# Seven-product SwiGLU pairs: silu and weight splits placed behind the PSUM copies in the queues of ScalarE and VectorE

## The chip, the cores and the metric

The kernel runs on one core of a Trainium2 chip. The metric is the device time of one execution in microseconds. A core has five engines with queues of their own, each working through its queue in order: TensorE (PE, with PEld for its weight loads), VectorE (DVE), ScalarE (ACT), GpSimd (POOL) and SyncE (SP), which issues the loads.

## What is computed

The program is two blocks of two layers each over 512 tokens of width 1024. The change concerns the four SwiGLU feed-forward networks of the second block (two per layer), with a hidden width of 22 chunks of 128:

```
def _swiglu(h, w_gu, w_down):
    gate, up = jnp.split(h @ w_gu, 2, axis=-1)
    return (jax.nn.silu(gate) * up) @ w_down

x = _layer_norm(alpha * x + 0.5 * _swiglu(x, ...), ...)
mix = _token_mixers(x, ...)
x = _layer_norm(alpha * x + mix, ...)
x = _layer_norm(alpha * x + 0.5 * _swiglu(x, ...), ...)
```

## The kernel before, in words

All matmuls run at three products per weight tile (`mm3`, L488 to L490): a float32 weight is split into a high part `wh`, cast by ScalarE, and a low part `wl`, the rest, subtracted by VectorE (`split`, L472 and L473). Tiles with an x, xs or p in their names are activations split in the same way.

`swiglu` goes over the 22 chunks in three parts of 8, 8 and 6. The first four chunks of a SwiGLU (five in the first one) are computed plainly. Each other chunk is a "pair" (`gated`): the gate and up products of one chunk for both halves of the tokens, taken together with seven products instead of eight. There are 71 pairs: parts of 3, 8 and 6 in the first SwiGLU and of 4, 8 and 6 in the three others. After a part, eight accumulations project its result down (L1141).

The weights of a pair come from `strassen_w`. SyncE loads two halves, ra (`raw`, tag wr, three buffers, shared with the loads of the projections) and rb (L991, tag wr2, two buffers). GpSimd makes four sums in order: L995 (p1 = a21 + a22), L996 (p2), L998 (p3), L999 (p4). The first two fill tile c1, the others c2 (both tag wc, two buffers in all). L995 needs rb and a free wc buffer. Four splits follow: 11/12 straight from ra, p2/p1 from c1 (`wh`, `wl`), p3/p4 from c2 (`wh2`, `wl2`) and 22 from rb (`wh3`, `wl3`, one buffer).

The products of a pair, twelve matmuls each, accumulate in three PSUM tiles R, Z and Q. Product 11 goes into R and ScalarE copies it to e1 (L1028). Product 12 goes into Z; VectorE adds e1 to it (add g1, L1032) and ScalarE takes silu (L1023). Product p2 goes on into R, copied to e2 (L1037). Product p1 goes into Q; p3 into R, copied to e3 (L1043); VectorE makes n2 of e3 and Q (L1045). Product 22 goes on into R (L1051), p4 into Q; then come add g2 (L1054), silu g2 (L1023), a multiplication (L1056) and the split of the result into ph and pl (L472, L473).

Two pairs are interleaved: the generator of a pair is stepped together with that of the one before, so that TensorE's order for a pair k with j before it is 11(k), 12(k), 22(j), p2(k), p1(k), p4(j), p3(k). A scheduler orders every queue by its own estimates and by edges that the code adds (`issue_after`: an instruction is queued behind another on the same engine). Before, such edges put the p2/p1 split behind add g1 and e2 of the pair before, and the p3/p4 split behind its e3 and n2.

Of the kernel before, what the change touches and what calls it, by code (L numbers as in the profile page):

```python
# [13 lines left out]
ALU = mybir.AluOpType  # L14
# [7 lines left out]
H = T // 2  # L22
# [332 lines left out]
class Prog:  # L355
# [156 lines left out]

    def mac(self, W, X, cols=slice(0, T), tag=None, off=None):

        ps = self.pt(tag=tag) if tag else self.acc()
        o = ps[:, : cols.stop - cols.start]
        if off is not None:
            self.nc.tensor.matmul(o, self.mean[:], off[:, cols], start=True, stop=False)
        for k, (wh, wl) in enumerate(W):
            self.mm3(o, wh, wl, X[k][0][:, cols], X[k][1][:, cols], k == 0 and off is None, k == len(W) - 1)  # L520
        return ps
# [445 lines left out]

        return X1, scale, X, finish

    def strassen_w(self, sa, sb, behind):  # L970


        nc = self.nc
        out = {}

        def put(names, src, tags, bufs=2, pool=None, behind=()):
            n = len(names) * 512
            hi, lo = ((pool or self.pool).tile([P, n], F32R, tag=t, name=self.nm(t), bufs=bufs) for t in tags)
            with ExitStack() as ctx:
                for ins in behind:  # L980
                    ctx.enter_context(self.tc.issue_after(ins))
                self.split(src, hi[:], lo[:])
            for i, name in enumerate(names):
                out[name] = [
                    (hi[:, c : c + P], lo[:, c : c + P]) for c in range(i * 512, i * 512 + 512, P)
                ]

        ra = self.raw(sa, 1024)
        put(("11", "12"), ra[:], ("wh", "wl"), pool=self.main)
        rb = self.pool.tile([P, 1024], F32, tag="wr2", name=self.nm("wr2"), bufs=2)  # L990
        nc.sync.dma_start(rb[:], sb)  # L991
        a11, a12, a21, a22 = ra[:, :512], ra[:, 512:], rb[:, :512], rb[:, 512:]
        c1, c2 = (self.pool.tile([P, 1024], F32, tag="wc", name=self.nm("wc"), bufs=2) for _ in range(2))
        p2, p1, p3, p4 = c1[:, :512], c1[:, 512:], c2[:, :512], c2[:, 512:]
        nc.gpsimd.tensor_tensor(p1, a21, a22, op=ALU.add)  # L995
        nc.gpsimd.tensor_tensor(p2, p1, a11, op=ALU.add)  # L996
        put(("p2", "p1"), c1[:], ("wh", "wl"), pool=self.main, behind=behind[0])
        nc.gpsimd.tensor_tensor(p3, a11, a21, op=ALU.add)  # L998
        nc.gpsimd.tensor_tensor(p4, p2, a12, op=ALU.add)  # L999
        put(("p3", "p4"), c2[:], ("wh2", "wl2"), behind=behind[1])  # L1000
        put(("22",), a22, ("wh3", "wl3"), 1)
        return out

    def prod(self, ps, W, X, start):

# [7 lines left out]
    def gated(self, X, srcs, mid, tags):  # L1013

        nc = self.nc
        tr, tq, tz = tags  # L1020
        gv, hv = self.scratch()
        g1, g2, e1, n2 = gv[:, :H], gv[:, H:], hv[:, :H], hv[:, H:]
        silu = lambda t: nc.scalar.activation(t, t, AF.Silu)  # L1023
        W = self.strassen_w(*srcs, self.behind)
        self.behind = behind = [[], []]
        R = self.pt(tag=next(tr))
        self.prod(R, W["11"], X["11"], True)
        nc.scalar.copy(e1, R[:, :H])  # L1028
        yield
        Z = self.pt(tag=next(tz))  # L1030
        self.prod(Z, W["12"], X["21"], True)
        behind[0].append(nc.vector.tensor_tensor(g1, e1, Z[:, :H], op=ALU.add).ins)  # L1032
        silu(g1)
        yield
        e2, e3 = (self.pool.tile([P, H], F32, tag="u", name=self.nm("u"), bufs=3)[:] for _ in range(2))
        self.prod(R, W["p2"], X["nf"], False)
        behind[0].append(nc.scalar.copy(e2, R[:, :H]).ins)  # L1037
        yield
        Q = self.pt(tag=next(tq))
        self.prod(Q, W["p1"], X["d"], True)  # L1040
        yield
        self.prod(R, W["p3"], X["t3"], False)
        behind[1].append(nc.scalar.copy(e3, R[:, :H]).ins)  # L1043
        behind[1].append(
            nc.vector.scalar_tensor_tensor(  # L1045
                out=n2, in0=e3, scalar=-1.0, in1=Q[:, :H], op0=ALU.mult, op1=ALU.subtract
            ).ins
        )
        yield
        self.prod(R, W["22"], X["t4"], False)  # L1050
        nc.vector.scalar_tensor_tensor(out=g1, in0=R[:, :H], scalar=-1.0, in1=g1, op0=ALU.mult, op1=ALU.mult)  # L1051
        yield
        self.prod(Q, W["p4"], X["22"], False)
        nc.vector.tensor_tensor(g2, e2, Q[:, :H], op=ALU.add)  # L1054
        silu(g2)
        nc.vector.tensor_tensor(g2, g2, n2, op=ALU.mult)  # L1056
        pair = self.xpair("m")
        self.split(gv[:], pair[0][:], pair[1][:])
        mid.append(pair)

    def plain(self, srcs, X, mid, normed):

        nc = self.nc
        sg, bc = {}, None

        def evac(i, ps, cols):
            j, n = i // 2, cols.stop - cols.start
            if bc is not None:
                t = self.t("up", tag="m")
                nc.vector.tensor_tensor(t[:, :n], ps[:, :n], bc[:, cols], op=ALU.mult)  # L1070
                ps = t
            if i % 2 == 0:
                if j not in sg:
                    sg[j] = self.t("sg", tag="m")
                nc.scalar.activation(sg[j][:, cols], ps[:, :n], AF.Silu)
            else:
                if j == len(mid):
                    mid.append(self.xpair("m"))
                g = sg[j][:, cols]
                nc.vector.tensor_tensor(g, ps[:, :n], g, op=ALU.mult)  # L1080
                self.split(g, mid[j][0][:, cols], mid[j][1][:, cols])

        if normed is not None:
            X1, scale, X, finish = normed
            for i, ps in self.lagged(srcs, X1, 2):
                if bc is None:
                    bc = scale()
                    self.tail = finish(bc)
                evac(i, ps, slice(0, T))
                next(self.tail, None)  # L1090
        else:
            W = [self.weights(srcs[i], KC, None if i < 2 else ("wh2", "wl2")) for i in range(4)]

            def product(W, ps, t):
                for k in range(KC):
                    self.mm3(ps, *W[k], *X.block(k, t), k == 0, k == KC - 1)

            for t, cols in enumerate(HALVES):
                for i in range(4):
                    ps = self.acc()  # L1100
                    product(W[i], ps[:, :H], t)
                    evac(i, ps, cols)
                    if t == 0:
                        next(self.tail, None)
            for i in range(4, len(srcs)):
                W = self.weights(srcs[i], KC)
                ps = self.acc()
                for t, cols in enumerate(HALVES):
                    product(W, ps[:, cols], t)
                evac(i, ps, slice(0, T))  # L1110
                next(self.tail, None)
        for _ in self.tail:
            pass
        self.behind = [self.last] * 2
        return X

    def swiglu(self, x, X, l, s, out=None, form=None, normed=None):


        nc, I = self.nc, self.I  # L1120
        wg = I[f"wg{l}{s}"]
        tags = cycle(("acc", "acc")), cycle(("s", "s")), cycle(("t", "t"))
        for a, b in PARTS:
            mid, j0 = [], a
            if a == 0:
                j0 = NPLAIN + (normed is not None)
                X = self.plain([wg[i * FC + j] for j in range(j0) for i in range(2)], X, mid, normed)
            before = iter(())
            for j in range(j0, b):
                g = self.gated(X, (wg[j], wg[FC + j]), mid, tags)  # L1130


                for one in (g, g, before, g, g, before, g):
                    next(one, None)
                before = g
            for _ in before:
                pass
            if b < FC:
                for nb in range(KC):
                    ps = self.proj(I[f"we{l}{s}"][nb][:, a * P : b * P], mid, b - a)  # L1140
                    nc.vector.scalar_tensor_tensor(  # L1141
                        out=x[nb][:], in0=ps[:], scalar=0.5 / ALPHA, in1=x[nb][:], op0=ALU.mult, op1=ALU.add
                    )
        return self.out_norm(
            x, lambda nb: I[f"we{l}{s}"][nb][:, a * P :], mid, 0.5 / ALPHA, l, 2 * s, out=out, form=form,
            wtag=("wh2", "wl2"),
        )
# [955 lines left out]
```

## Time and profile before

| | |
|---|---|
| median of three runs | 3385.3 us (3382.5 to 3385.59) |
| profiled execution | 3384.03 us |
| its span | 3382.2 us, mean granted clock 0.987 |
| TensorE busy | 3272.4 us (97%) |
| VectorE busy | 2290.7 us (68%) |
| ScalarE busy | 1587.1 us (47%) |
| GpSimd busy | 875.3 us (26%) |

Shares are of the span. They average over stages of different kinds; the pairs of the four SwiGLUs are only some of them. Matmuls overlap, so that TensorE's busy time is that in which it had at least one matmul in work.

### The profile page before, as it was taken

The page shows a single profiled execution, that of the slowest core. Times are in us where ns is not written, and L with a number is a line of the kernel's source. Part 1 is how long each engine was busy: PE and PEld are TensorE (multiplying, and loading weights), DVE is VectorE, ACT ScalarE, POOL GpSimd, SP SyncE. Part 2 cuts the span into 40 slices and gives each one's busy share as a digit, 9 for nine tenths or more (in the row PEclk, how much of TensorE's full clock was granted, in tenths as well). Part 3 has the DMA queues.
Part 4 walks back from the last instruction along what each step waited for, and adds up shares of the span by engine and source line. Part 5 has one row for each costly group of instructions (what it writes and reads, how often), then busy time and mean ns, then how long its engine had stood idle before and what let it go on. Part 6 is the DMA issues. An engine that isn't in the chain of part 4 may idle for free.

```text
span 3382.2 us, 47780 instructions
## 1 busy us (share of the span) xinstructions
PE 3272.4 (97%) x18386; PEld 2761.4 (82%) x18386; DVE 2290.7 (68%) x3708; ACT 1587.1 (47%) x3012; POOL 875.3 (26%) x635
## 2 busy tenths in 40 slices
PE   8999999998999999999999999999999999999998
PEld 6777888886788887899867798998998877789987
DVE  7866664648664647666677886668666767896666
ACT  6423443436442434344466653445443456754534
POOL 3111110114110104344200153444353410043534
PEclk9999999999999999999999999999999999999999
DMA  3321223231233323232312123222323322023232
GB/s 117 90 60 57 88 88 105 86 114 57 94 94 94 95 87 99 94 100 85 100 54 69 59 86 100 100 89 93 100 94 100 100 63 78 29 89 112 86 101 70
DMA packets 101109, 293.79 MB, mean 87 GB/s; under 512 B 20240, under 2 KB 26640, under 8 KB 100624
## 3 DMA queue, kind: packets, MB, share of 16 engines
q1 hardware_dynamic: 100880, 290.73, 27.4%
q8 instruction: 144, 2.36, 0.3%
q14 instruction: 85, 0.70, 0.1%
HBM read 280.20 MB, written 2.62 MB: 84 GB/s over the span
## 4 chain that ended last, share of the span: by engine, by line
PE 67%; DVE 13%; POOL 7%; issue 4%; ACT 4%; DMA 3%; SPq 0%; POOLq 0%; ACTq 0%; DVEq 0%
PE psacc L488 15%; PE psacc L490 14%; PE psacc L489 14%; PE pss L488 3%; DMA wr<-wg 3%; PE pss L490 3%; PE pss L489 3%; DVE wl L466 2%; PE pst L489 2%; PE pst L490 2%; PE pst L488 2%; POOL wc L996 2%; POOL wc L999 2%; POOL wc L995 1%; PE pst L1688 1%
## 5 line engine op out<-in xcount | busy, mean ns | idle before, releaser
L488 PE MATMUL psacc<-xh,wh 128*128 128x512 f32 (+1 forms) x1977 | 725.6, 369 | 36.1 <-ACT u L1043 12.1
L465 ACT ACTIVATE wh<-wr 128x512 fp32r<-128x512 f32 (+2 forms) x760 | 435.1, 611 | 643.0 <-PE psacc L489 379.2
L490 PE MATMUL psacc<-xh,wl 128*128 128x512 f32 (+1 forms) x1977 | 716.5, 363 | 12.1 <-DVE wl L466 9.6
L489 PE MATMUL psacc<-xl,wh 128*128 128x512 f32 (+1 forms) x1977 | 717.9, 364 | 2.9 <-DVE xl L590 1.5
L466 DVE TENSOR_TENSOR wl<-wr,wh 128x512 fp32r<-128x512 f32 (+2 forms) x760 | 581.1, 796 | 199.4 <-ACT wh L465 186.5
L488 PEld LDWEIGHTS psacc<-xh,wh 128*128 128x128 f32 x1977 | 377.4, 192 | 114.3 <-ACT u L1043 20.9
L490 PEld LDWEIGHTS psacc<-xh,wl 128*128 128x128 f32 x1977 | 377.5, 191 | 76.6 <-DVE wl L466 12.2
L489 PEld LDWEIGHTS psacc<-xl,wh 128*128 128x128 f32 x1977 | 376.9, 191 | 66.6 <-DVE xl L590 4.9
L488 PE MATMUL psacc<-ph,wh 128*128 128x512 f32 (+1 forms) x774 | 303.6, 393 | 5.5 <-DVE xs L473 2.2
L490 PE MATMUL psacc<-ph,wl 128*128 128x512 f32 (+1 forms) x774 | 303.6, 393 | 2.0 <-DVE wl L466 2.0
L489 PE MATMUL psacc<-pl,wh 128*128 128x512 f32 (+1 forms) x774 | 304.4, 393 | 0.4 <-DVE pl L939 0.3
L473 DVE TENSOR_TENSOR wl<-wc,wh 128x1024 fp32r<-128x1024 f32 x142 | 191.0, 1345 | 159.6 <-ACT wh L472 159.6
L472 ACT ACTIVATE wh<-wc 128x1024 fp32r<-128x1024 f32 x142 | 150.7, 1062 | 203.7 <-POOL wc L996 88.5
L653 POOL TENSOR_TENSOR cv<-cv,cv 128x512 f32<-128x512 f32 x44 | 57.3, 1303 | 542.7 <-DVE cv L644 517.6
L490 PE MATMUL psacc<-xs,wl 128*128 128x256 f32 (+1 forms) x671 | 194.6, 290 | 0.0
L488 PE MATMUL psacc<-xs,wh 128*128 128x256 f32 (+1 forms) x671 | 194.6, 290 | 0.0
L489 PE MATMUL psacc<-xs,wh 128*128 128x256 f32 (+1 forms) x671 | 194.1, 289 | 0.0
L473 DVE TENSOR_TENSOR wl<-wr,wh 128x512 fp32r<-128x512 f32 (+1 forms) x142 | 181.2, 1303 | 12.6 <-ACT wh L472 12.2
L488 PEld LDWEIGHTS psacc<-ph,wh 128*128 128x128 f32 x774 | 146.5, 189 | 39.2 <-issue 3.4
L490 PEld LDWEIGHTS psacc<-ph,wl 128*128 128x128 f32 x774 | 146.9, 190 | 34.4 <-DVE wl L466 2.4
L489 PEld LDWEIGHTS psacc<-pl,wh 128*128 128x128 f32 x774 | 146.9, 190 | 33.1 <-DVE pl L939 1.2
L995 POOL TENSOR_TENSOR wc<-wr 128x512 f32<-128x512 f32 x71 | 97.8, 1377 | 286.8 <-DMA wr<-wg 115.6
(546 smaller groups left out, 7508.3 us busy)
## 6 DMA issues: line engine op xcount, KB each, us to landing
wr<-wg SPq DMA_DIRECT2D x176, 512.0 KB, 3.8
wr<-wu SPq DMA_DIRECT2D x88, 512.0 KB, 3.6
wr<-we SPq DMA_DIRECT2D x64, 512.0 KB, 3.5
wr<-wd SPq DMA_DIRECT2D x32, 512.0 KB, 3.6
wr<-we SPq DMA_DIRECT2D x32, 384.0 KB, 3.1
wr<-wi SPq DMA_DIRECT2D x22, 512.0 KB, 3.6
wr<-w_ret SPq DMA_DIRECT2D x16, 512.0 KB, 3.6
wr<-wl_in SPq DMA_DIRECT2D x16, 512.0 KB, 3.6
```

Of the source, the lines that this page charges most:

```text
L465: one = nc.scalar.activation(hi[:, a:b], raw[:, a:b], AF.Copy)
L466: two = nc.vector.tensor_tensor(lo[:, a:b], raw[:, a:b], hi[:, a:b].bitcast(F32), op=ALU.subtract)
L472: nc.scalar.activation(hi, src, AF.Copy)
L473: nc.vector.tensor_tensor(lo, src, hi.bitcast(F32), op=ALU.subtract)
L488: nc.tensor.matmul(ps, wh, xh, start=start, stop=False, **kw)
L489: nc.tensor.matmul(ps, wh, xl, start=False, stop=False, **kw)
L490: nc.tensor.matmul(ps, wl, xh, start=False, stop=stop, **kw)
L653: nc.gpsimd.tensor_tensor(gate[:], gate[:], val[:], op=ALU.mult)
L995: nc.gpsimd.tensor_tensor(p1, a21, a22, op=ALU.add)
L996: nc.gpsimd.tensor_tensor(p2, p1, a11, op=ALU.add)
L999: nc.gpsimd.tensor_tensor(p4, p2, a12, op=ALU.add)
L1688: nc.tensor.transpose(pt[:, qb * P : (qb + 1) * P], t[:, kb * P - k0 : (kb + 1) * P - k0], self.ident)
```

## The change

`strassen_w` becomes a generator: `gated` sends it the instructions behind which the next split is queued. The p2/p1 split goes behind e2 and add g1 of the pair before,; the p3/p4 split behind the pair's own e1 and add g1; the split of 22 behind its own e2. Silu g1 is queued behind e2. The end of a pair (silu g2, the multiplication, the split of the result) becomes a step of its own, and silu g2 is queued behind the e3 copy of the latest pair. The loop of `swiglu` steps the pair before once more.

```diff
--- before.py
+++ after.py
@@ -967,7 +967,15 @@
 
         return X1, scale, X, finish
 
-    def strassen_w(self, sa, sb, behind):
+    def queued(self, behind):
+
+        ctx = ExitStack()
+        for ins in behind:
+            ctx.enter_context(self.tc.issue_after(ins))
+        return ctx
+
+    def strassen_w(self, sa, sb):
+
 
 
         nc = self.nc
@@ -976,9 +984,7 @@
         def put(names, src, tags, bufs=2, pool=None, behind=()):
             n = len(names) * 512
             hi, lo = ((pool or self.pool).tile([P, n], F32R, tag=t, name=self.nm(t), bufs=bufs) for t in tags)
-            with ExitStack() as ctx:
-                for ins in behind:
-                    ctx.enter_context(self.tc.issue_after(ins))
+            with self.queued(behind):
                 self.split(src, hi[:], lo[:])
             for i, name in enumerate(names):
                 out[name] = [
@@ -994,12 +1000,15 @@
         p2, p1, p3, p4 = c1[:, :512], c1[:, 512:], c2[:, :512], c2[:, 512:]
         nc.gpsimd.tensor_tensor(p1, a21, a22, op=ALU.add)
         nc.gpsimd.tensor_tensor(p2, p1, a11, op=ALU.add)
-        put(("p2", "p1"), c1[:], ("wh", "wl"), pool=self.main, behind=behind[0])
+        behind = yield out
+        put(("p2", "p1"), c1[:], ("wh", "wl"), pool=self.main, behind=behind)
         nc.gpsimd.tensor_tensor(p3, a11, a21, op=ALU.add)
         nc.gpsimd.tensor_tensor(p4, p2, a12, op=ALU.add)
-        put(("p3", "p4"), c2[:], ("wh2", "wl2"), behind=behind[1])
-        put(("22",), a22, ("wh3", "wl3"), 1)
-        return out
+        behind = yield
+        put(("p3", "p4"), c2[:], ("wh2", "wl2"), behind=behind)
+        behind = yield
+        put(("22",), a22, ("wh3", "wl3"), 1, behind=behind)
+        yield
 
     def prod(self, ps, W, X, start):
 
@@ -1021,38 +1030,42 @@
         gv, hv = self.scratch()
         g1, g2, e1, n2 = gv[:, :H], gv[:, H:], hv[:, :H], hv[:, H:]
         silu = lambda t: nc.scalar.activation(t, t, AF.Silu)
-        W = self.strassen_w(*srcs, self.behind)
-        self.behind = behind = [[], []]
+        weights = self.strassen_w(*srcs)
+        W = next(weights)
+        weights.send(self.behind)
         R = self.pt(tag=next(tr))
         self.prod(R, W["11"], X["11"], True)
-        nc.scalar.copy(e1, R[:, :H])
+        one = nc.scalar.copy(e1, R[:, :H]).ins
         yield
         Z = self.pt(tag=next(tz))
         self.prod(Z, W["12"], X["21"], True)
-        behind[0].append(nc.vector.tensor_tensor(g1, e1, Z[:, :H], op=ALU.add).ins)
-        silu(g1)
+        add = nc.vector.tensor_tensor(g1, e1, Z[:, :H], op=ALU.add).ins
+        weights.send((one, add))
         yield
         e2, e3 = (self.pool.tile([P, H], F32, tag="u", name=self.nm("u"), bufs=3)[:] for _ in range(2))
         self.prod(R, W["p2"], X["nf"], False)
-        behind[0].append(nc.scalar.copy(e2, R[:, :H]).ins)
+        two = nc.scalar.copy(e2, R[:, :H]).ins
+        self.behind = (two, add)
+        with self.queued((two,)):
+            silu(g1)
+        weights.send((two,))
         yield
         Q = self.pt(tag=next(tq))
         self.prod(Q, W["p1"], X["d"], True)
         yield
         self.prod(R, W["p3"], X["t3"], False)
-        behind[1].append(nc.scalar.copy(e3, R[:, :H]).ins)
-        behind[1].append(
-            nc.vector.scalar_tensor_tensor(
-                out=n2, in0=e3, scalar=-1.0, in1=Q[:, :H], op0=ALU.mult, op1=ALU.subtract
-            ).ins
-        )
+        self.third = nc.scalar.copy(e3, R[:, :H]).ins
+        nc.vector.scalar_tensor_tensor(out=n2, in0=e3, scalar=-1.0, in1=Q[:, :H], op0=ALU.mult, op1=ALU.subtract)
         yield
         self.prod(R, W["22"], X["t4"], False)
         nc.vector.scalar_tensor_tensor(out=g1, in0=R[:, :H], scalar=-1.0, in1=g1, op0=ALU.mult, op1=ALU.mult)
         yield
         self.prod(Q, W["p4"], X["22"], False)
         nc.vector.tensor_tensor(g2, e2, Q[:, :H], op=ALU.add)
-        silu(g2)
+        yield
+
+        with self.queued((self.third,)):
+            silu(g2)
         nc.vector.tensor_tensor(g2, g2, n2, op=ALU.mult)
         pair = self.xpair("m")
         self.split(gv[:], pair[0][:], pair[1][:])
@@ -1111,7 +1124,7 @@
                 next(self.tail, None)
         for _ in self.tail:
             pass
-        self.behind = [self.last] * 2
+        self.behind = self.last
         return X
 
     def swiglu(self, x, X, l, s, out=None, form=None, normed=None):
@@ -1130,7 +1143,7 @@
                 g = self.gated(X, (wg[j], wg[FC + j]), mid, tags)
 
 
-                for one in (g, g, before, g, g, before, g):
+                for one in (g, g, before, g, g, before, g, before):
                     next(one, None)
                 before = g
             for _ in before:
```

The queues of a steady-state pair change on ScalarE. These are seven rows in the second part of the first SwiGLU, first as they stand before; e1 is the copy into g_1989, e3 the copy into u_1984 (u_1982 in the second piece), and g_1946 holds the result of the pair before.

```order
L472 ACTIVATE wh_1996_11223<-wc_1994_11219 128x1024
L1023 ACTIVATE g_1946_10947<-g_1946_10947 128x256
L1043 COPY u_1984_11149<-psacc_1981_11106 128x256
L472 ACTIVATE wh2_1998_11229<-wc_1995_11220 128x1024
L472 ACTIVATE ph_1986_11191<-g_1946_10947 128x512
L1028 COPY g_1989_11210<-psacc_2002_11237 128x256
L472 ACTIVATE wh_2012_11344<-wr_2011_11342 128x1024
```

The same seven places of ScalarE's queue after the change:

```order
L472 ACTIVATE wh_1996_11223<-wc_1994_11219 128x1024
L1057 COPY u_1982_11144<-psacc_1977_11098 128x256
L1032 ACTIVATE g_1946_10947<-g_1946_10947 128x256
L472 ACTIVATE ph_1986_11205<-g_1946_10947 128x512
L1038 COPY g_1989_11210<-psacc_1998_11229 128x256
L472 ACTIVATE wh2_2000_11257<-wc_1995_11220 128x1024
L472 ACTIVATE wh_2012_11344<-wr_2011_11342 128x1024
```

The e3 copy moved ahead of silu of g_1946, and the e1 copy ahead of the cast wh2.

At the start of the second part SyncE's queue changes. Here wr is ra and wr2 is rb; wr_1929, wr_1948 and wr_1969 belong to the first three pairs of the part, and wr2_1972 is the third pair's.

```order
L448 DMA wr_1929_10850<-wg00 128x1024
L991 DMA wr2_1972_11086<-wg00 128x1024
L448 DMA wr_1948_10949<-wg00 128x1024
L448 DMA wr_1969_11080<-wg00 128x1024
L448 DMA wr_1990_11211<-wg00 128x1024
L448 DMA wr_2011_11342<-wg00 128x1024
L448 DMA wr_2032_11473<-wg00 128x1024
L991 DMA wr2_1993_11217<-wg00 128x1024
```

SyncE's queue at the same places after the change:

```order
L448 DMA wr_1929_10850<-wg00 128x1024
L448 DMA wr_1948_10949<-wg00 128x1024
L448 DMA wr_1969_11080<-wg00 128x1024
L448 DMA wr_1990_11211<-wg00 128x1024
L448 DMA wr_2011_11342<-wg00 128x1024
L997 DMA wr2_1972_11086<-wg00 128x1024
L448 DMA wr_2032_11473<-wg00 128x1024
L997 DMA wr2_1993_11217<-wg00 128x1024
```

The third pair's rb load moved from behind the first pair's ra load to behind the fifth pair's, wr_2011, whose buffer is that of the second pair's ra.

On VectorE the end of the projections and the first pair of the same part read like this; h is the projection's result, wc_1933 is c1 and wc_1934 is c2 of the first pair, and wl_1950 is the second pair's.

```order
L466 TENSOR_TENSOR wl_1921_10782<-wr_1919_10780,wh_1920_10781 128x512 x2
L473 TENSOR_TENSOR wl2_1938_10869<-wc_1934_10859,wh2_1937_10868 128x1024
L1141 SCALAR_TENSOR_TENSOR h_6_69<-psacc_1918_10754,h_6_69 128x512
L466 TENSOR_TENSOR wl_1925_10816<-wr_1923_10814,wh_1924_10815 128x512 x2
L1141 SCALAR_TENSOR_TENSOR h_7_70<-pss_1922_10788,h_7_70 128x512
L473 TENSOR_TENSOR wl_1931_10853<-wr_1929_10850,wh_1930_10852 128x1024
L1141 SCALAR_TENSOR_TENSOR h_8_71<-pss_1926_10822,h_8_71 128x512
L473 TENSOR_TENSOR wl_1936_10863<-wc_1933_10858,wh_1935_10862 128x1024
L1032 TENSOR_TENSOR g_1927_10848<-g_1928_10849,pst_1942_10890 128x256
```

VectorE's queue there after the change:

```order
L466 TENSOR_TENSOR wl_1925_10816<-wr_1923_10814,wh_1924_10815 128x512 x2
L1154 SCALAR_TENSOR_TENSOR h_7_70<-pss_1922_10788,h_7_70 128x512
L473 TENSOR_TENSOR wl_1931_10853<-wr_1929_10850,wh_1930_10852 128x1024
L1154 SCALAR_TENSOR_TENSOR h_8_71<-pss_1926_10822,h_8_71 128x512
L473 TENSOR_TENSOR wl_1936_10863<-wc_1933_10858,wh_1935_10862 128x1024
L1042 TENSOR_TENSOR g_1927_10848<-g_1928_10849,pst_1938_10882 128x256
L473 TENSOR_TENSOR wl2_1940_10897<-wc_1934_10859,wh2_1939_10896 128x1024
L473 TENSOR_TENSOR wl_1950_10952<-wr_1948_10949,wh_1949_10951 128x1024
L473 TENSOR_TENSOR wl3_1944_10917<-wr2_1932_10856,wh3_1943_10916 128x512
```

The subtract wl2 of the first pair moved from among the projections to behind the p2/p1 subtract (wl_1936) and add g1; the subtract wl3 of the same pair, before the change in the part before, comes here too.

## Rows read from the trace of the kernel before

**Rows 1.** The page, its first line.

```profile
span 3382.2 us, 47780 instructions
```

**Rows 2.** Waits of TensorE: engine, line, releaser: us in total, times, longest us.

```profile
PE psacc L488 <- ACT u L1043: 12.1, 22, 2.1
...
PE psacc L488 <- ACT g L1028: 7.9, 23, 1.9
```

**Rows 3.** Seventh pair's window: us; busy PE, PEld, DVE, ACT, POOL; PEclk; DMA; GB/s.

```profile
1479.04:1490.26 11.22, 10.39 (x86) 9.99 (x84) 6.72 (x11) 5.74 (x12) 6.07 (x4) 1.00 0.27 92
```

**Rows 4.** Timeline of TensorE: start, us, instruction [idle before <- releaser].

```profile
1352.42 0.39 PE L488 MATMUL psacc<-xh,wh 128*128 128x256 f32 x1 [1.87 <-ACT g L1028]
...
1353.65 0.58 PE L490 MATMUL psacc<-xh,wl 128*128 128x256 f32 x1 [0.72 <-DVE wl L473]
...
1447.68 0.28 PE L488 MATMUL psacc<-xh,wh 128*128 128x256 f32 x1
...
1457.53 0.28 PE L488 MATMUL psacc<-xh,wh 128*128 128x256 f32 x1
...
1490.66 0.38 PE L488 MATMUL psacc<-xh,wh 128*128 128x256 f32 x1 [0.27 <-ACT g L1028]
...
1501.95 0.38 PE L488 MATMUL psacc<-xh,wh 128*128 128x256 f32 x1 [0.28 <-ACT g L1028]
```

**Rows 5.** Timeline of ScalarE, seventh pair.

```profile
1485.29 1.06 ACT L472 ACTIVATE wh<-wc 128x1024 fp32r<-128x1024 f32 x1 [3.25 <-POOL wc L996]
1487.97 0.42 ACT L1023 ACTIVATE g<-g 128x256 f32<-128x256 f32 x1 [1.62 <-DVE g L1054]
1488.29 0.35 ACT L1043 COPY u<-psacc 128x256 f32<-128x256 f32 x1
1488.77 1.06 ACT L472 ACTIVATE wh<-wc 128x1024 fp32r<-128x1024 f32 x1
1489.74 0.62 ACT L472 ACTIVATE ph<-g 128x512 fp32r<-128x512 f32 x1
1490.26 0.35 ACT L1028 COPY g<-psacc 128x256 f32<-128x256 f32 x1
```

**Rows 6.** Timeline of GpSimd, seventh pair's L999, then the eighth's first sums.

```profile
1486.47 2.27 POOL L999 TENSOR_TENSOR wc<-wc,wr 128x512 f32<-128x512 f32 x1
1493.86 1.29 POOL L995 TENSOR_TENSOR wc<-wr 128x512 f32<-128x512 f32 x1 [5.12 <-DVE wl L473]
1495.23 1.29 POOL L996 TENSOR_TENSOR wc<-wc,wr 128x512 f32<-128x512 f32 x1
```

**Rows 7.** Timeline of SyncE: third pair's rb load, then two loads, seventh pair.

```profile
1413.05 0.33 SPq L991 DMA_DIRECT2D wr<-wg  x1
...
1488.76 0.33 SPq L462 DMA_DIRECT2D wr<-we  x1
1489.21 0.36 SPq L991 DMA_DIRECT2D wr<-wg  x1
```

**Rows 8.** Timeline of VectorE, seventh pair.

```profile
1486.38 1.23 DVE L473 TENSOR_TENSOR wl<-wc,wh 128x1024 fp32r<-128x1024 f32 x1 [3.50 <-ACT wh L472]
1487.52 0.41 DVE L1054 TENSOR_TENSOR g<-u,pss 128x256 f32<-128x256 f32 x1
1488.42 0.60 DVE L1056 TENSOR_TENSOR g<-g,g 128x256 f32<-128x256 f32 x1 [0.48 <-ACT g L1023]
...
1489.86 1.23 DVE L473 TENSOR_TENSOR wl<-wc,wh 128x1024 fp32r<-128x1024 f32 x1 [0.51 <-ACT wh L472]
```

**Rows 9.** Timeline of VectorE, first pair of the second part.

```profile
1427.63 1.23 DVE L473 TENSOR_TENSOR wl<-wc,wh 128x1024 fp32r<-128x1024 f32 x1 [0.17 <-ACT wh L472]
```

**Rows 10.** Timeline of GpSimd: second pair's first sum, then the third pair's.

```profile
1417.16 1.29 POOL L995 TENSOR_TENSOR wc<-wr 128x512 f32<-128x512 f32 x1 [2.43 <-DVE wl L473]
...
1434.86 1.29 POOL L995 TENSOR_TENSOR wc<-wr 128x512 f32<-128x512 f32 x1 [3.39 <-issue]
...
1440.58 1.75 POOL L999 TENSOR_TENSOR wc<-wc,wr 128x512 f32<-128x512 f32 x1
```

## The prediction

> **What bounds the kernel now.** I read the page first: the span is 3382.2 us [rows 1], and the execution it comes from took 3384.03 us, so 1.8 us lie around the span; the median of the three runs is 1.3 us higher, which is nothing beside the terms below. Then TensorE's waits: the two that the change aims at are p3's wait for the e3 copy (L1043), 12.1 us in 22 waits, and p2's wait for the e1 copy (L1028), 7.9 us in 23 [rows 2]. All the change could remove directly is thus 20 us of 3382.
>
> The question is what those waits stand for. I take one late pair, the seventh of the second part of the first SwiGLU (that part has 8 pairs; I count them first to eighth). Its stretch of 11.22 us has TensorE busy for 10.39 us at a granted clock of 1.00 [rows 3], so 0.83 us are idle. In the rows of TensorE the idle time before p2 of the seventh pair is put to the e1 copy [rows 4], and ScalarE's rows show why: silu g2 at 1487.97, the e3 copy at 1488.29, the cast wh2 of p3/p4 at 1488.77, ph at 1489.74, e1 at 1490.26 [rows 5]. The cast wh2 needs GpSimd's last sum (L999), which ends at 1486.47 + 2.27 = 1488.74 [rows 6]. So the queue order makes e1 late only because L999 is late.
>
> Why is L999 late? SyncE issues the load of ra that reuses the buffer L999 has read at 1488.76, 0.02 us after that end, and the next pair's rb load at 1489.21 [rows 7]; 4.65 us later, at 1493.86, that pair's first sum L995 starts [rows 6]. The row names a VectorE subtract as what ended its wait, but the last subtract of the pair's sums ended at 1489.86 + 1.23 = 1491.09 [rows 8], 2.8 us earlier, so it is the landing of rb. Four sums later the circle closes. I measure its period at w, the start of the cast of p2/p1, which comes right behind L996. For the seventh pair w is 1485.29 [rows 5], for the eighth 1493.86 + 1.37 + 1.29 + 0.04 = 1496.56 [rows 6]: 11.27 us. That is the 11.22 us of TensorE's stretch. Late pairs run at the pace of this circle (L999, SyncE, the landing, four sums), and neither silu nor a PSUM copy stands in it. A shorter wait on one line comes back on another.
>
> **The change part by part.** The instructions are the same; three things move.
>
> First, ScalarE in the steady state: e3 ahead of silu g2, e1 ahead of wh2. Working from w of the seventh pair with the durations of before: the subtract starts at w + 1.09, add g2 at w + 2.23, silu g2 at w + 2.68, the multiply at w + 3.13 and ends at w + 3.73 [rows 5, 8]; ph takes 0.62, to w + 4.35; e1, now right behind it, 0.35, to about w + 4.68 with the same small gap that p2 shows. Before, p2 starts at 1490.66 [rows 4], which is w + 5.37. So the reorder gives 0.69 us of phase against the circle once per part, and nothing per pair, because the circle's period does not change: SyncE's order in the steady state is the same.
>
> Second, the first pair of each part: its cast and subtract of p3/p4 (1.06 us on ScalarE, 1.23 us on VectorE [rows 5, 8]) and of 22 (half that width) move from the end of the part before to behind its own e1 and e2. Their own cost I put at nothing, since ScalarE and VectorE have idle time there. But they hold buffers. The second pair's c1 takes the buffer that comes free first: before it was the first pair's c2, freed by the early wl2, so L995 ran at 1417.16 [rows 10]. Now it is the first pair's c1, which is free when the p2/p1 subtract ends, 1427.63 + 1.23 = 1428.86 [rows 9]. So before, two of the second pair's four sums were still to do at 1428.94; now all four are.
>
> Third, the rb load of the third pair. Before it was issued at 1413.05, early [rows 7]; now SyncE's queue has it behind the ra load that waits for the second pair's L999. This is in all 12 parts. Now the sum. Four sums beside busy VectorE take, by the third pair's rows (1434.86 to 1440.58 + 1.75), 7.47 us [rows 10]; alone they take 4 x 1.29 plus a small gap, 5.3 us (two rows of the eighth pair show 1.29) [rows 6]. I take 7.47, because the four now stand beside the subtracts that were moved there. L999 of the second pair then ends at 1428.94 + 7.47 = 1436.41; rb is issued 0.47 us later as in the late pairs [rows 6, 7], at 1436.88, and L995 of the third starts at 1441.53 instead of 1434.86 [rows 10]. Its w is 1441.53 + 2.70 = 1444.23, and p2 can start at w + 4.68 = 1448.91; before it started at 1447.68 [rows 4]. The part now runs on the circle from the third pair on, where before it had slack to use up first: of the 6.67 us by which the third L995 moves, p2 sees 1.23, so 5.4 us were slack. The eighth pair: w = 1444.23 + 5 x 11.27 = 1500.58, p2 at 1505.26 against 1501.95 [rows 4], 3.3 us late. At the part's end the last pair no longer has its e3 wait, about half of which (0.3 us) I take back: +3.0. A six-pair part gives the same, since by the sixth pair before is on the circle too. There are 8 such parts: +24. In the four-pair parts the fourth pair's p2 comes at 1444.23 + 11.27 + 4.68 = 1460.18 against 1457.53 [rows 4]: +2.65, three times, +8. The one three-pair part gains: its e1 wait of 1.87 us [rows 4], where e1 stood behind wh2, goes, and 0.72 us before its third matmul: -2.6. Sum: 24 + 8 - 2.6 = +29.4, or 3384.0 + 29.4 = 3413.
>
> Bounds: with sums at 5.3 us each of the 11 parts is 2.2 us better, +5.4 in all. From the other side, L999 takes 2.27 us where a 1.23 us subtract of VectorE (1486.38 to 1487.61) runs beside it, and 1.29 us alone [rows 6, 8]: 0.98 us more. If three subtracts of 1.23 us and one of half the width (0.62) add all of their time to 4 x 1.29, the four sums take 9.5 us and each part is 2.0 us worse: 29.4 + 22 = +51. The Trainium skill, "SBUF — State Buffer", section "Who interferes with whom", says that a VectorE instruction with two SBUF inputs and a GpSimd instruction that reads SBUF block one another for a whole instruction. By that rule the sum would stand at the +51 end; the trace's 0.98 us for 1.14 us of overlap agrees nearly with it.
>
> **Rivals.** (A) Faster. The queue order itself is the limit and the third pair's late load is hidden: both waits go, 12.1 + 7.9, and the time is 3364. For it: the waits are real, and ScalarE is in idle stretches while silu waits. Against it: the circle of 11.27 us without ScalarE in it, and the slack of 5.4 us being less than the 6.67 us by which the third L995 moves. It decides if that L995 moves by less than 5.4 us, that is if the four sums take about 5.3 us (a move of 4.5), and if in addition the circle shortens by 0.3 us per pair (20 us over 71 pairs) once the copies leave the way. (B) Uncontended sums: the lower bound, +5.4, 3389. For it: GpSimd often shows 1.29. Against it: the third pair's rows. (C) Full blocking: +51, 3435. For it: 0.98 us per overlap. Against it: the third pair's 7.47 us has the same neighbours and is less than 9.5.
>
> **How the numbers follow.** Forecast 3413 with a chance of 0.60, its own range 3398 to 3427; A 0.16; B 0.10; C 0.14. Under 0.2% of the time (6.8 us) a measurement can't be told from no change, so faster is A, 0.16; the same is B, 0.10; slower the rest, 0.74. The range leaves out most of A and the upper half of C: 3377 to 3433.
>
> **What would show it.** Right: in the changed kernel p3's wait for the e3 copy (12.1 us now) is nearly gone, while p2's wait for e1 has grown well beyond 7.9 us, over 1 us in each late pair; the third pair's rb load is issued just behind the second pair's last sum; the third pair's first sum starts 13.9 us behind the start of the first pair's p2/p1 subtract, 1441.53 - 1427.63, instead of 7.2; late pairs still take 11.0 to 11.3 us. Wrong: late pairs at about 10 us, which would make the queue order the limit (A); or the third pair's first sum less than 11.8 us behind that subtract, which would leave the delay nearly inside the slack (B).

## The result and the profile after

The changed kernel takes 3419.8 us (median of 4 runs, 3419.0 to 3422.2) against 3383.9 us before (4 runs): the ratio is 1.011, with a 95% interval of 1.0097 to 1.0123. It is 36 us slower; forecast were 29. The profiled execution has a span of 3417.2 us, where before had 3382.2 [rows 1]. TensorE's waits for the two PSUM copies (engine, line, releaser: us in total, times, longest) now read

```profile
PE psacc L488 <- ACT g L1038: 61.9, 47, 1.7
...
PE psacc L488 <- ACT u L1057: 0.3, 1, 0.3
```

They answer to [rows 2], where e3 (now L1057) had 12.1 us and e1 (now L1038) 7.9 us. The wait for e3 is gone, as the change meant it, and the wait for e1 is eight times as long. A reader who saw only this would put the blame on e1, which now stands behind silu g2 and ph. These are ScalarE's rows of a late pair after (start, us, instruction, idle time before and its releaser), with the same work as [rows 5]:

```profile
1483.41 1.06 ACT L472 ACTIVATE wh<-wc 128x1024 fp32r<-128x1024 f32 x1 [3.83 <-POOL wc L1002]
1484.38 0.35 ACT L1057 COPY u<-psacc 128x256 f32<-128x256 f32 x1
1486.10 0.42 ACT L1032 ACTIVATE g<-g 128x256 f32<-128x256 f32 x1 [1.37 <-DVE g L1064]
1487.20 0.63 ACT L472 ACTIVATE ph<-g 128x512 fp32r<-128x512 f32 x1 [0.68 <-DVE g L1069]
1487.73 0.35 ACT L1038 COPY g<-psacc 128x256 f32<-128x256 f32 x1
```

ScalarE is idle for 3.83 us before the cast of p2/p1, and what ends that is GpSimd's second sum. So the delay reaches ScalarE through GpSimd, and what stands between the cast and e1 carries it on; the first experiment tests this reading. Back to the start of the same part: GpSimd's rows after, the second pair's four sums and the first ones of the third and fourth pair, answer to [rows 10]:

```profile
1422.24 1.30 POOL L1001 TENSOR_TENSOR wc<-wr 128x512 f32<-128x512 f32 x1 [14.36 <-issue]
1423.62 2.15 POOL L1002 TENSOR_TENSOR wc<-wc,wr 128x512 f32<-128x512 f32 x1
1425.73 2.27 POOL L1005 TENSOR_TENSOR wc<-wr,wr 128x512 f32<-128x512 f32 x1
1427.95 1.75 POOL L1006 TENSOR_TENSOR wc<-wc,wr 128x512 f32<-128x512 f32 x1
1434.64 1.29 POOL L1001 TENSOR_TENSOR wc<-wr 128x512 f32<-128x512 f32 x1 [4.94 <-DVE wl L473]
...
1445.83 1.62 POOL L1001 TENSOR_TENSOR wc<-wr 128x512 f32<-128x512 f32 x1 [5.02 <-DVE wl L473]
```

SyncE issues the third pair's rb load (answering to the first of [rows 7]) 0.41 us behind the end of the second pair's last sum, 1427.95 + 1.75 = 1429.70; the pair of loads below it repeats with every late pair:

```profile
1430.11 0.42 SPq L997 DMA_DIRECT2D wr<-wg  x1
1440.84 0.33 SPq L448 DMA_DIRECT2D wr<-wg  x1
1441.22 0.42 SPq L997 DMA_DIRECT2D wr<-wg  x1
```

VectorE's p2/p1 subtract of the first pair, from which the forecast measured (compare [rows 9]):

```profile
1420.88 1.22 DVE L473 TENSOR_TENSOR wl<-wc,wh 128x1024 fp32r<-128x1024 f32 x1 [0.21 <-ACT wh L472]
```

Two of TensorE's rows, p2 of the third and of the eighth pair (compare [rows 4]):

```profile
1442.07 0.38 PE L488 MATMUL psacc<-xh,wh 128*128 128x256 f32 x1 [1.02 <-ACT g L1038]
...
1499.67 0.38 PE L488 MATMUL psacc<-xh,wh 128*128 128x256 f32 x1 [1.42 <-ACT g L1038]
```

The third pair's first sum starts 13.8 us behind that subtract's start (7.2 before). From the third pair on every pair of the part waits for e1 (1.02 us, then 1.41 or 1.42 us each), where before the waits, for e3 and e1, began only with the fourth pair's p3 and came to 0.49 to 0.89 us a pair.

### The profile page after: what moved, and what is told of

Same layout as the page of the kernel before. It is cut to its first block, busy times and chain, and to the rows that moved or that the text cites. A ratio compares the mean times of both kernels' runs of the same rounds, so it can differ in the third digit from the quotient of the medians.

```text
span 3417.2 us, 47771 instructions
## 1 busy us (share of the span) xinstructions
PE 3265.8 (96%) x18386; PEld 2755.7 (81%) x18386; DVE 2261.8 (66%) x3708; ACT 1577.8 (46%) x3012; POOL 878.2 (26%) x635
## 4 chain that ended last, share of the span: by engine, by line
PE 61%; DVE 14%; POOL 10%; issue 7%; DMA 5%; ACT 4%; SPq 0%; POOLq 0%; DVEq 0%; ACTq 0%
PE psacc L488 14%; PE psacc L490 13%; PE psacc L489 13%; DMA wr<-wg 4%; PE pss L488 3%; PE pss L490 2%; PE pss L489 2%; POOL wc L1001 2%; POOL wc L1002 2%; POOL wc L1006 2%; DVE wl L473 2%; DVE wl L466 2%; POOL wc L1005 1%; PE pst L1701 1%; PE pst L489 1%
## 5 line engine op out<-in xcount | busy, mean ns | idle before, releaser
L466 DVE TENSOR_TENSOR wl<-wr,wh 128x512 fp32r<-128x512 f32 (+2 forms) x760 | 567.2, 778 | 194.1 <-ACT wh L465 180.9
L1001 POOL TENSOR_TENSOR wc<-wr 128x512 f32<-128x512 f32 x71 | 107.1, 1508 | 427.6 <-issue 150.3
L473 DVE TENSOR_TENSOR wl<-wr,wh 128x512 fp32r<-128x512 f32 (+1 forms) x142 | 163.4, 1184 | 8.9 <-ACT wh L472 8.9
```

The costliest lines, as they stand in the source:

```text
L466: two = nc.vector.tensor_tensor(lo[:, a:b], raw[:, a:b], hi[:, a:b].bitcast(F32), op=ALU.subtract)
L473: nc.vector.tensor_tensor(lo, src, hi.bitcast(F32), op=ALU.subtract)
```

## The experiments

The table has two lengths read from the starts of the e1 copies in the second part of the first SwiGLU (8 pairs): from the first to the third pair, and the mean of the five pairs from the third to the eighth. Ratios are against the kernel before on the same chip; between chips its median moved from 3382.5 to 3384.2 us. "rb ahead" marks kernels with the extra edge on SyncE that the third experiment introduces. The diffs of this section are shortened.

| kernel | median us | ratio (95%) | first to third | mean late pair |
|---|---|---|---|---|
| before | 3383.9 | | 17.65 | 11.14 |
| after | 3419.8 | 1.0097 to 1.0123 | 20.26 | 11.52 |
| 1: reorder of later pairs only | 3382.7 | 0.9988 to 1.0006 | 17.53 | 11.37 |
| 2: late first-pair splits only | 3428.2 | 1.0119 to 1.0147 | 21.91 | 11.01 |
| 3: before, rb ahead of ra | 3381.5 | 0.9984 to 1.0001 | 17.65 | 11.03 |
| 4: after, rb ahead of ra | 3388.0 | 1.0012 to 1.0030 | 19.39 | 10.95 |
| 5: after, only p3/p4 split late | 3398.5 | 1.0036 to 1.0066 | 19.47 | 11.37 |
| 6: after, only 22 split late | 3398.3 | 1.0034 to 1.0064 | 18.24 | 11.55 |
| 7: before, sums on VectorE, rb ahead | 3351.6 | 0.9893 to 0.9923 | 19.17 | 9.55 |
| 8: before, two sums on VectorE, rb ahead | 3360.2 | 0.9919 to 0.9949 | 17.41 | 10.48 |
| 9: after, sums on VectorE | 3339.6 | 0.9857 to 0.9890 | 17.72 | 9.98 |
| 10: reorder only, sums on VectorE, rb ahead | 3348.3 | 0.9880 to 0.9912 | 17.33 | 10.10 |

**The change in two halves.** The first kernel has only the reorder in the later pairs: the first pair of a part sends all its splits at once, behind what they stood behind before.

```diff
+        if first:
+            weights.send(self.behind2)  # p3/p4: behind e3 and n2 of the pair before
+            weights.send(())            # 22
```

> The changed kernel, but the first pair of each part keeps its p3/p4 and 22 splits where they stood before; so the orders of SyncE and GpSimd are those of the kernel before, and only the queues of ScalarE and VectorE within the later pairs are new. Theory (the loss comes from the first pair's splits, which make the second pair's sums and the third pair's rb load late; the late pairs run at the pace of the circle of L999, SyncE, landing, sums): about 3376 to 3388 us, e1 waits of about 1.5 us in late pairs all the same, since those are idle time of the circle. Rival (e1 behind silu g2 and ph is itself the cost, 62 us of waits on it): about 3415 us or more.

It takes 3382.7 us, no difference from before, and shows e1 waits all the same (the copy is L1044 there):

```profile
PE psacc L491 <- ACT g L1044: 30.6, 25, 2.8
```

The wait for e3 (12.1 us before) is gone there, and the 30.6 us are 23 more than e1 had before, 10.6 more than both had together. They stand for no lost time; what makes the pairs take 11 us lies elsewhere. The second kernel is the other half: old queues in the later pairs, and the first pair's splits late.

```diff
         weights.send(self.behind)
+        if not first:
+            weights.send(self.behind2)
+            weights.send(())
...
         add = nc.vector.tensor_tensor(g1, e1, Z[:, :H], op=ALU.add).ins
+        silu(g1)
...
-        with self.queued((two,)):
-            silu(g1)
...
         nc.vector.tensor_tensor(g2, e2, Q[:, :H], op=ALU.add)
-        yield
-        with self.queued((self.third,)):
-            silu(g2)
+        silu(g2)
```

> The kernel before, with only the first pair's splits of each part moved behind its own e1 and e2 as in the change; the later pairs keep the old queues. Theory: the whole loss is there without the 0.7 us of phase that the reorder gives, 3410 to 3424 us, with e3 and e1 waits split over two lines as before. Rival (the reorder of the later pairs is the cost): about 3384 us.

It takes 3428.2 us, 45 us more than before, a little over the range. All of the loss is in the first pair's splits, and beside them the reorder takes some 8 us off again. The forecast gave it 0.69 us of phase in each of 11 parts, 7.6 us, but the trace does not confirm that term: the two profiled executions are 11.1 us apart, of which 5.6 lie ahead of the first pair, where the kernels are alike, and the 5.5 behind it are uneven, 1.0 us in a 4-pair part, 0.5 in an 8-pair and 0.1 in a 6-pair one. On its lines this kernel looks quite unlike the changed one: its waits are for e3 (L1068 there), not for e1 (L1044).

```profile
PE psacc L491 <- ACT u L1068: 41.4, 38, 3.2
...
PE psacc L491 <- ACT g L1044: 7.3, 27, 0.3
```

**The two steps of the loss apart.** The fifth kernel keeps only the p3/p4 split of the first pair late, so that the rb load of the third pair is early and only c1's buffer is late; the sixth keeps only its split of 22 late, so that the sums of the second pair are early and only the rb load is late.

```diff
+        if first: put(("22",), a22, ("wh3", "wl3"), 1)        # fifth
+        if first: weights.send(self.behind2)                   # sixth: p3/p4 at once
```

> The changed kernel, but the first pair's split of 22 stands early again; only its p3/p4 split is late. So the second pair's first sum still waits for the late buffer, while the third pair's rb load is early again. Theory: the two steps of the sum need each other. The second pair's L999 is 5 us later, but the third pair's sums follow at once, about 1 us later than before, and the slack takes that: 3380 to 3392 us. Rival (the second pair's sums beside the subtracts are the cost): 3405 us or more.

> The changed kernel, but the first pair's p3/p4 split stands early again; only its split of 22 is late. So the second pair's sums are early, and the third pair's rb load stands behind the ra load that waits for the second pair's L999. Theory (each step alone is mostly taken by slack): the third pair's first sum moves about 2 us, 3382 to 3398 us. Rival (the place of the rb load in SyncE's queue is the whole cost): 3410 us or more.

Each costs 14 us, more than expected for the fifth and just over the range for the sixth; together they cost 36, somewhat more than the two costs added up (28). Each alone moves the third pair (19.47 and 18.24 us from the first, 17.65 before), both together move it to 20.26. So neither is the whole cost, both rivals fall, and the slack took less than I thought.

**What the late pairs wait for.** The third and fourth kernel put one edge on SyncE: an ra load that waits for a pair's last sum stands behind the next pair's rb load.

```diff
+        with self.queued((self.rbs[pair + 1],)):   # pair: whose ra buffer is taken
             self.nc.sync.dma_start(dst, src)
```

> The kernel before, with one edge on SyncE: an ra load that must wait for a pair's L999 is queued behind the next pair's rb load instead of ahead of it. Nothing else moves. Theory (the circle through SyncE bounds the late pairs): late pairs fall from 11.0 to 11.3 us to 9.9 to 10.3 us, the waits for e3 and e1 nearly vanish without any change on ScalarE, 3350 to 3362 us. Rival (ScalarE's and VectorE's queues bound the late pairs): late pairs stay above 11 us, about 3384 us.

> The changed kernel with the same edge on SyncE. Theory: the third pair's late start stays (about 1 us a part), the late pairs fall from 11.5 to about 10 us, so that the changed kernel gets below the kernel before: 3350 to 3375 us. Rival (e1 behind silu g2 and ph bounds the pairs): e1 waits of over 1 us stay, 3410 us or more.

The fourth is a miss: some 31 of the 36 us come back, so most of the loss goes by way of the order of the loads, but the kernel stays 5 us above before (on the same chip) and does not get below it, as I had expected. The third refutes what I had claimed for it: with the circle through SyncE open, late pairs still take 11.03 us, and the time is the same. These are the numbers of its rival, and VectorE is indeed in it: TensorE's largest wait on a pair is now for the multiplication behind product 22 (L1082 there), which stands in VectorE's queue behind two subtracts.

```profile
PE psacc L499 <- DVE g L1082: 14.4, 21, 1.0
```

The third kernel's window of a late pair shows why (us; busy of TensorE, its loads, VectorE, ScalarE and GpSimd; clock; DMA share; GB/s), beside [rows 3]:

```profile
1480.83:1491.95 11.12, 10.86 (x91) 10.62 (x90) 10.17 (x11) 5.53 (x11) 8.46 (x5) 1.00 0.29 104
```

VectorE is busy for 10.17 us of such a pair, where it had 6.72 with as many instructions. Its rows in this window (the splits are L484):

```profile
1480.45 1.23 DVE L484 TENSOR_TENSOR wl<-wc,wh 128x1024 fp32r<-128x1024 f32 x1 [0.46 <-ACT wh L483]
1481.59 1.78 DVE L484 TENSOR_TENSOR pl<-g,ph 128x512 fp32r<-128x512 f32 x1
1483.30 0.41 DVE L1057 TENSOR_TENSOR g<-g,pst 128x256 f32<-128x256 f32 x1
1483.63 3.69 DVE L484 TENSOR_TENSOR wl<-wr,wh 128x1024 fp32r<-128x1024 f32 x2
1487.24 0.41 DVE L1082 SCALAR_TENSOR_TENSOR g<-psacc,g 128x256 f32<-128x256 f32 x1
1487.57 1.96 DVE L484 TENSOR_TENSOR wl<-wc,wh 128x1024 fp32r<-128x1024 f32 x1
```

And GpSimd's four sums at the same time (L1013 to L1018):

```profile
1480.51 2.32 POOL L1013 TENSOR_TENSOR wc<-wr 128x512 f32<-128x512 f32 x1 [4.11 <-DMA wr<-wg]
1482.90 1.62 POOL L1014 TENSOR_TENSOR wc<-wc,wr 128x512 f32<-128x512 f32 x1
1484.48 2.28 POOL L1017 TENSOR_TENSOR wc<-wr,wr 128x512 f32<-128x512 f32 x1
1486.73 1.72 POOL L1018 TENSOR_TENSOR wc<-wc,wr 128x512 f32<-128x512 f32 x1
```

The two subtracts that take 1.82 us alone take 3.69, the pl subtract 1.78 instead of 0.69, the subtract of 1.23 takes 1.96; the four sums take 7.9 us instead of 5.2. The instructions that read two tiles in SBUF stretch beside a sum, while those with a PSUM operand (0.41 us) don't. The subtract at 1480.45 keeps its 1.23 us, since it was there first; the sum that starts beside it takes 2.32 us, 1.08 until the next row of VectorE and 1.24 behind that, nearly the 1.29 us of a sum alone. Over the whole kernel VectorE is busy for 2383.7 us against 2290.7. The sums start some 4 us earlier against the pair's e1, and so fall beside the subtracts. If the two kinds never run side by side, a pair needs 5 subtracts, one multiplication of two tiles in SBUF (3 x 1.23 + 2 x 0.69 + 0.42) and four sums (5.16), 10.65 us by the times that they take alone: nearly the 11.0 us measured. (The multiplication's 0.60 us in [rows 8] fall beside the last sum; in the seventh kernel below, without sums on GpSimd, its median is 0.42.) So there are two limits close to one another, the circle at about 11.3 us and this one at about 10.7 to 11, and opening one only shows the other. The Trainium skill, "SBUF — State Buffer", section "Who interferes with whom", says that such instructions of the two engines block one another; the rows agree.

**Taking the overlap away.** The seventh kernel has the four sums on VectorE, the eighth only p3 and p4.

```diff
-        nc.gpsimd.tensor_tensor(p1, a21, a22, op=ALU.add)
+        nc.vector.tensor_tensor(p1, a21, a22, op=ALU.add)
```

(and p2, p3 and p4 in the same way). Both keep the third kernel's edge, so the third kernel is what they compare with. The ninth, below, has the sums on VectorE without that edge, and in its late pairs rb stands ahead of ra all the same (issued at 1452.58 and 1453.18).

> The kernel before with rb ahead of ra in SyncE's queue (as in the third experiment) and all four sums of a pair on VectorE instead of GpSimd. The third experiment left late pairs at 11.0 to 11.1 us with VectorE busy for 10.1 us of each instead of 6.7, at the same instructions. Theory (subtracts and sums hold one another up when they run side by side): with the sums on VectorE the subtracts go back to 1.23 us, VectorE is busy for 6.7 plus four sums of 0.6 to 0.8 us, about 9.5 us, and late pairs take 9.9 to 10.4 us: 3345 to 3365 us. Rival (VectorE is simply full): the sums come on top, late pairs over 12 us, 3420 us or more.

> As the run before, but only the last two sums (p3 and p4) on VectorE, and the first two on GpSimd. Theory: half of the overlap is gone, VectorE busy 8.5 to 9.3 us of a late pair, 10.2 to 10.8 us per pair, 3355 to 3375 us. Rival (VectorE is full): over 3400 us.

Both times come out as the theory has it, 3351.6 and 3360.2 us, and the late pairs nearly (9.85 and 10.48 us). VectorE's share does not: in a late pair of the seventh it is busy for 8.67 us where about 9.5 were expected, in one of the eighth for 9.4 to 9.8 us where 8.5 to 9.3 were. The window of a late pair in the seventh, and some of VectorE's rows in it:

```profile
1470.68:1480.53 9.85, 9.85 (x86) 9.85 (x85) 8.67 (x15) 5.86 (x12) 0.00 (x0) 1.00 0.30 106
```

```profile
1471.79 0.68 DVE L484 TENSOR_TENSOR pl<-g,ph 128x512 fp32r<-128x512 f32 x1
...
1472.72 0.68 DVE L1017 TENSOR_TENSOR wc<-wr,wr 128x512 f32<-128x512 f32 x1
1473.33 1.82 DVE L484 TENSOR_TENSOR wl<-wr,wh 128x1024 fp32r<-128x1024 f32 x2
```

TensorE is busy all of the 9.85 us, the subtracts are back at their old times (the table's 9.55 us is less than 9.85, since the third pair there makes up for a long second one), and a sum takes 0.68 us instead of 1.29 to 2.3. VectorE, with four instructions more, is busy for less time than in the third kernel. No line of e1 or e3 with more than 0.4 us is left among TensorE's waits. Two things change at once here, though: the overlap is gone, and each sum is shorter than it was alone on GpSimd (0.68 against 1.29 us). No run separates them.

**The change on top of that.** The ninth kernel is the changed one with the sums on VectorE, the tenth has only the reorder of the later pairs with them.

> The changed kernel with all four sums on VectorE. The seventh experiment, the kernel before with that, had 3351.6 us and late pairs of 9.85 us with TensorE never idle. Theory (the change costs only because late pairs ran at a pace slower than TensorE's, so that a late start was never made up): with TensorE as the limit and the sums at 0.69 us, the first pair's late splits are taken by slack, 3346 to 3358 us. Rival (the late first-pair splits cost by themselves): 36 us above 3351.6, about 3388 us.

> The reorder of the later pairs alone (first pair's splits early, as in the first experiment) with all four sums on VectorE. Theory (the reorder only shifts waits that come from elsewhere): no difference from the seventh experiment, 3346 to 3357 us. Rival (with the other limit gone the copies that come earlier pay): 12 to 20 us below it, 3332 to 3340 us.

The ninth takes 3339.6 us: the late first-pair splits cost nothing now, the rival is out, and the result is below the range that I gave. It has the lowest median of all, 1.3% under the kernel before. Its interval lies just below that of the seventh and overlaps that of the tenth; whether a gain stands behind the further 0.3% stays open. The tenth can't be told from the seventh. So the same edit costs 36 us with the old order of loads, 6.5 us with rb ahead (the fourth against the third kernel), and nothing where the late pairs keep TensorE's pace.

## Why the prediction was right, point by point

**The mechanism at a part's start** came out nearly to the tenth. The four sums of the second pair were put at 7.47 us and took 7.46 (1422.24 to 1429.70). From the start of the first pair's p2/p1 subtract to the third pair's first sum 13.9 us were forecast, and 13.76 measured. From the cast of p2/p1 to p2 4.68 us were forecast; in the late pair above the cast is at 1483.41 and p2 at 1488.14, 4.73 us. From the first e1 of the part (1428.19 before, 1421.40 after) to the third pair's p2 the forecast has 20.72 us and the trace 20.67. The first, second, fifth and sixth experiment confirm that the loss is in these two steps and not in the reorder.

One row was misread without harm: the load at 1488.76 in [rows 7], called ra's, is one of the projections' (wr<-we), which takes the same buffer.

**The late pairs' pace** was the term that was mis-sized. The forecast kept 11.27 us and named 11.0 to 11.3 as a sign of being right; after it is 11.52. GpSimd's first sum shows why, one line of the page of before and one of after (busy, mean ns; idle before):

```profile
L995 POOL TENSOR_TENSOR wc<-wr 128x512 f32<-128x512 f32 x71 | 97.8, 1377 | 286.8 <-DMA wr<-wg 115.6
```

```profile
L1001 POOL TENSOR_TENSOR wc<-wr 128x512 f32<-128x512 f32 x71 | 107.1, 1508 | 427.6 <-issue 150.3
```

In the late pairs of after this sum takes 1.5 to 1.7 us, since it starts while VectorE still subtracts (in the eighth pair the sum starts at 1491.86, and two subtracts end at 1492.38); before it mostly took 1.29 (1493.86, [rows 6], and the same two subtracts had ended at 1493.76). The sum stands in the circle, so each late pair is longer. The eighth pair's p2 came 78.27 us behind the first e1, where 77.07 were forecast and 73.76 stood before. Over the whole: the four 8-pair parts lost 17.5 us and the four 6-pair parts 14.3 (each from its first e1 to the next part's or the kernel's end; 24 forecast for the eight), the three 4-pair parts 10.0 (8 forecast), and the 3-pair part gained 2.3 (2.6 forecast; from the cast of its first pair's 11 and 12, since its first e1 itself moves). That is +39.5 us against +29.4. The profiled executions differ by 35.0, because the stretch ahead of that cast, where no order changes, was 4.5 us shorter in the one of after; over the eight profiled kernels with the sums on GpSimd that cast starts anywhere from 1338.12 to 1344.80.

**What bounds the late pairs** was only half right. The circle through SyncE does set the pace of before and after, and a shorter wait on one line did come back on another. But the prediction spoke as if it were the one limit. The third experiment shows a second one right behind it, and that one I had only as the price of rival C for the sums at a part's start, not as a limit of the steady state. The forecast hung on it only by the pace: the 0.25 us that each late pair is longer are a sum beside a subtract.

**The rivals.** A, that the removed waits would be a gain, is refuted by the first experiment: the reorder alone brings nothing. B falls with the time. C, full blocking, would have had 9.5 us for the second pair's sums; they took 7.46. That does not speak against blocking itself. C put the whole wait on GpSimd, and VectorE bore a part of it: beside these sums its subtracts read

```profile
1423.22 1.40 DVE L473 TENSOR_TENSOR wl<-wc,wh 128x1024 fp32r<-128x1024 f32 x1
1424.54 4.01 DVE L473 TENSOR_TENSOR wl<-wr,wh 128x1024 fp32r<-128x1024 f32 x2
1428.47 2.31 DVE L473 TENSOR_TENSOR wl<-wc,wh 128x1024 fp32r<-128x1024 f32 x1
```

where they take 1.23, 1.82 and 1.23 us alone.

## What to carry to other kernels

Find the loop that sets a stage's pace before pricing a wait: the largest wait on a PSUM copy was 12, 31, 41 or 62 us in four of these kernels, and it told nothing of their times (3384, 3383, 3428 and 3420 us; the second largest belongs to the slowest). Where a split or a load is moved to a later place, ask which buffer it frees, which load stands behind that in the queue, and whether the stage has any slack left to make up a late start; the same edit costs 1.1% with the sums on GpSimd, 0.2% once rb is loaded ahead of ra, and nothing with the sums on VectorE. And when opening a limit brings nothing, look for the engine whose busy time rose at the same count of instructions.

## What the runs showed of the hardware that was not expected

Moving all 284 sums of 128x512 from GpSimd to VectorE, the busier engine, made the kernel 1% faster: they take 0.68 us there instead of 1.29 alone and up to 2.3 beside a subtract, and VectorE's busy time rises only from 2290.7 to 2334.0 us. Bringing the same sums forward by some 4 us while they stayed on GpSimd raised VectorE's busy time by more, 93 us, with no instruction added.
